# A hybrid decoder layer: the output projection split after six recurrent pairs, and the decode state update moved into the second feed-forward

## The chip, the cores and the metric

The kernel runs on one core of a Trainium2 chip. Its engines work side by side, each with its own in-order queue: TensorE (matmuls; PE in the profile, PEld its weight loads), the vector engine (DVE), the scalar engine (ACT), GpSimd (POOL) and SyncE (SP), which here issues nearly all transfers from HBM. The metric is the device time of one execution in microseconds; lower is better.

## What is computed

One layer is applied to 256 prompt tokens and to 8 decode tokens, 264 columns in all, with a model width of 2048:

```
x = x + 0.5 * swiglu(rmsnorm(x), first feed-forward)      # width 5504
proj = rmsnorm(x) @ w_in
o_att  = sliding-window attention, 16 heads, 4 key/value heads
o_rwkv = RWKV-7 time mixing, 16 heads of 64
x = x + concat(o_att, o_rwkv) @ w_out                     # 2048 x 2048
x = x + 0.5 * swiglu(rmsnorm(x), second feed-forward)
y = rmsnorm(x)
```

For the 8 decode tokens each RWKV head holds a 64 x 64 state that is read, updated once and returned:

```
sa = S @ (-kk)
S  = S * exp(logw) + outer(sa, kk * a) + outer(v, k)
```

The read `sa` and the head's output are needed for `o_rwkv`; the new S is only an output of the layer (`new_wkv_sample`).

## The kernel before

Everything is float32. A matmul is made exact enough by splitting each operand into a rounded part `hi` and a rest `lo`: three matmuls of 128x128 weights against 128x264 activations per tile (hi*hi, hi*lo, lo*hi). Weights come as chunks of up to four k-tiles, 128x512 (`chunk`, called by `gemm`): SP loads `raw` (L122, ring of 6), ACT rounds it to `hi` (L123), the vector engine subtracts to `lo` (through the helper at L58; rings of 4 for `hi` and `lo`). A chunk of four k-tiles feeds 12 matmuls. The helpers `tt` (L58), `stt` (L61), `ts` (L65), `act` (L68) and `mm` (L74) issue most instructions, so their lines stand for many places in the code.

Each feed-forward goes through its 43 blocks of 128 hidden columns in six parts of 8, 7, 7, 7, 7 and 7 (`PARTS`). A part first computes gate and up for its blocks (96 matmuls a block), then adds its share of the down projection for all 16 output tiles. After each block the vector engine evacuates two accumulators, ACT takes SiLU, and POOL does a product and a subtraction of 128x264 (the vector engine does them for the last block of a part).

The mixing stage (`mixing_body`) streams `w_in` and drives many generators, the tasks, between its chunks: `gemm` calls `tick` after each chunk, and every task then issues its next step. There are tasks for the preparation of each of eight recurrent head pairs (`prep`), for the chain of each batch of two pairs (`chain`), for each pair of attention heads (`attend`), for the decode attention (`dec_attend`), and for the decode state update (`dec_state`). The results of the eight pairs and of the eight attention tiles are 16 k-tiles of the output projection, in `mixed`.

The output projection runs in two passes over its 16 output tiles. `PASS` names the k-tiles of each pass: pairs 0 to 7, then attention tiles 8 to 15. Before a pass `drain` advances the tasks until those that it needs are done; in the first pass the attention tasks go on between its chunks. Each pass adds its result to the residual `xr`, and each k-tile is split into `hi` and `lo` by `split` (even tiles subtract on POOL, odd ones on the vector engine). Before the last `drain` the eight decode columns of the attention tiles are copied in by POOL (L824).

`dec_state` is spawned before the first pass. It transposes the decode vectors out of `XD` (matmuls `m<-C,XD`) into `XR`, and then goes through the 64 x 64 states of all heads in 16 blocks of 128x256: load a block of S on SP, five operations of 128x256 (two on POOL, three on the vector engine), store it on SP (L684). `drain([dst])` waits for it at the end of mixing.

The order in each engine's queue isn't the program's order. The tile layer takes all operations with their dependencies and builds each queue with a planner that plays the work through on its own clock: an operation that is ready there, on an engine that is free there, goes in, with earlier program order and `high_priority` first. Weight chunks and splits have high priority.

Of the kernel before, what the change touches and what calls it, by code (L numbers as in the profile page):

```python
# [7 lines left out]
F32 = mybir.dt.float32  # L8
# [5 lines left out]
P = 128  # L14
# [22 lines left out]
LKV = 26  # L37
SEQ = [('b', 0), ('b', 1), ('b', 2), ('b', 3), ('kv', 0), ('kv', 1), ('kv', 2), ('kv', 3), ('q', 0), ('q', 1), ('q', 2), ('q', 3), ('q', 4), ('q', 5), ('q', 6), ('q', 7)]
NSO = (12, 13)
PASS = [[0, 1, 2, 3, 4, 5, 6, 7], [8, 9, 10, 11, 12, 13, 14, 15]]  # L40

VG1, VGM, VG2, VGF = 0, 16, 32, 48
VMU, VKK, VKA, VA0, VRK, VLW, VLB, VSK, VSD = 64, 90, 98, 106, 114, 122, 130, 138, 154
# [4 lines left out]
def body(tc, I, O):  # L48
# [8 lines left out]
    def tt(e, out, a, b, op):  # L57
        return e.tensor_tensor(out=out, in0=a, in1=b, op=op)  # L58
# [11 lines left out]
    def bc(ap, shape):  # L70
        return ap.broadcast_to(list(shape))

    def mm(out, lhsT, rhs, start=True, stop=True, **k):
        TE.matmul(out, lhsT, rhs, start=start, stop=stop, **k)  # L74
# [8 lines left out]
    def drain(only, hold=()):  # L83
        while any(g in only for g in tasks):
            tick(hold)

    def spawn(g):
        tasks.append(g)
        return g
# [5 lines left out]
    with ExitStack() as ctx:  # L95
# [10 lines left out]
        def tmp(shape=(P, T), dt=F32):  # L106
            pool, n = cur[0]
            return pool.tile(list(shape), dt, tag="t", bufs=n, name=uid("t"))
# [4 lines left out]
        def mp():  # L113
            return pp.tile([P, 512], F32, tag="m", bufs=NM, name=uid("m"))
# [87 lines left out]
        def copy_one():  # L202
            n, c, b = copies.pop()
            tc.keep_in_program_order(A.dma_start(O[n][b, 0:127, :], I[c][b, 1:128, :]))

        def ffn(nrm, xr, gu, dn, nxt, load, begin=False):
            rstd = None
            f0 = 0
            for pi, nf in enumerate(PARTS):
                hs = [None] * nf  # L210
                late = []
                if begin:
                    early(pi)
                first = pi == 0
                if first:
                    banks = [acc() for _ in range(NACC)] + [mp() for _ in range(NM)]
                    n0 = len(banks) // 2
                    for k in range(CH):
                        load(k)
                    for k0 in range(0, KD, CH):  # L220
                        xs = nrm.xs + [None] * (KD - len(nrm.xs))
                        for i, ps in enumerate(banks):
                            gemm(ps, gu[i // 2, i % 2], xs, rng=(k0,), ahead=False)
                            if i >= len(banks) - CH and k0 + CH < KD:
                                load(k0 + CH + i - len(banks) + CH)
                    for f in range(n0):
                        raw = [tmp(), tmp()]
                        V.tensor_copy(raw[0], banks[2 * f][:, :T])
                        A.copy(raw[1], banks[2 * f + 1][:, :T])
                        late.append((f, *raw))  # L230
                for f in range(f0 + n0 if first else f0, f0 + nf):
                    pgu = [acc(), acc()]
                    if first and f == n0:
                        sq = iter(range(KD))

                        def step():
                            for k in [x for _, x in zip(range(2), sq)]:
                                nrm.square(xr[k], k % 2, True)
                    else:
                        step = None  # L240
                    if begin and pi and copies:
                        copy_one()
                    for ps, w in zip(pgu, (gu[f, 0], gu[f, 1])):
                        gemm(ps, w, nrm.xs, step)
                    last = f == f0 + nf - 1
                    if rstd is None:
                        rstd = nrm.rstd(tmp())
                    late.append((f, *(x[:, :T] for x in pgu)))
                    now = [late.pop()]
                    for _ in range(len(late) if last else min(len(late), 2 if first and f == n0 + 1 else 1)):  # L250
                        now.append(late.pop(0))
                    for j, pg, pu in now:
                        E = V if last else G
                        g = tmp()
                        tt(V, g, pg, rstd, ALU.mult)
                        s = tmp()
                        act(s, g, AF.Silu)
                        u = tmp()
                        tt(V, u, pu, rstd, ALU.mult)
                        tt(E, u, u, s, ALU.mult)  # L260
                        hi, lo = tmp(dt=F32R), tmp(dt=F32R)
                        A.copy(hi, u)
                        tt(E, lo, u, hi.bitcast(F32), ALU.subtract)
                        hs[j - f0] = (hi, lo)
                if pi == len(PARTS) - 1:
                    nrm.xs = None
                for o in range(KD):
                    ps = acc()
                    gemm(ps, dn[o, :, f0 * P:(f0 + nf) * P], hs)
                    stt(xr[o], ps[:, :T], 0.5, xr[o], ALU.mult, ALU.add)  # L270
                    if pi == len(PARTS) - 1:
                        nxt(o)
                f0 += nf
# [19 lines left out]
                    xr += [xg[:, j] for j in range(4)]  # L293
                ffn(n1, xr, I["gu1"], I["dn1"], nxt, load, True)

        def mixing(n2, n3):
            with tc.tile_pool(name="mx", bufs=1) as mx:
                cur[0] = (mx, NT)
                return mixing_body(mx, n2, n3)

        def mixing_body(mx, n2, n3):
            def fix(shape, name):
                return mx.tile(list(shape), F32, name=name)

# [3 lines left out]
            def load(src, shape):  # L308
                t = ring(shape, "ld", NLD)
                SP.dma_start(t, src)  # L310
                return t
# [1 line left out]
            ident, bo, cm = C[:, CID:CID + P], C[:, CBO:CBO + P], C[:, CCM:CCM + P]  # L313
            tri, msk = C[:, CTR:CTR + P], C[:, CMK:CMK + P]
            shc = fix((P, NSH, NB + 1), "shc")
            XD = fix((P, 8, NPAIR, NB), "XD")
            wc = fix((P, NPAIR, 4), "wc")
            tw = fix((65, T), "tw")
            G.memset(tw[64:65, :], 1.0)
# [6 lines left out]
            ts(V, nmu, mu, -1.0, ALU.mult, 1.0, ALU.add)  # L326
            tt(V, ss, ss, bc(mu.unsqueeze(2), (P, NSH, NB)), ALU.mult)
            qd = fix((P, 2, NB, 4), "qd")
            XR = fix((P, 5, 64), "XR")
            nbat = len(BATCH)  # L330
            scr = [dp.tile([BATCH[b] * 16, 1024], F32, tag=f"sa{b}", name=f"sa{b}") for b in range(nbat)]
            scr2 = [dp.tile([BATCH[b] * 16, 1024], F32, tag=f"sb{b}", name=f"sb{b}") for b in range(nbat)]
# [323 lines left out]
                tt(V, y, yp[:, :T], r, ALU.mult)  # L656
                yield

            def dec_state():
                while any(g.left for g in bts):  # L660
                    yield
                ps = mp()
                for i in range(5):
                    for h in range(2):
                        r = HALF[h]
                        mm(ps[r, i * 64:i * 64 + 64], XD[r, i, :, :], ident[r, r])
                A.copy(XR, ps[:, :320].rearrange("p (c t) -> p c t", c=5))
                yield
                n = 4
                shp = (P, n, 64)  # L670

                def bj(i):
                    return bc(XR[:, i:i + 1, :], shp)

                for k in range(64 // n):
                    r = slice(k * n, k * n + n)
                    S = load(I["st"][:, r, :], shp)
                    t1, t2 = tmp(shp), tmp(shp)
                    tt(G, t1, bc(XR[:, 3, r].unsqueeze(2), shp), bj(4), ALU.mult)
                    tt(V, S, S, bj(1), ALU.mult)  # L680
                    tt(V, t2, bc(XR[:, 0, r].unsqueeze(2), shp), bj(2), ALU.mult)
                    tt(V, S, S, t2, ALU.subtract)
                    tt(G, S, S, t1, ALU.add)
                    SP.dma_start(O["wkvs"][:, r, :], S)  # L684
                    yield

            kT, vT, Vt = [None] * 2, [None] * 2, [None] * 2
            kvn = [None] * 2

# [182 lines left out]
            k0 = 0  # L872
            for pi, ks in enumerate(PASS):
                drain(need(ks), att if max(ks) < 8 else ())
                if pi == 0:
                    dst = spawn(dec_state())
                with tc.high_priority():
                    for k in ks:
                        split(k)
                for o in range(KD):  # L880
                    ps = acc()
                    gemm(ps, I["wout"][o, :, k0 * P:(k0 + len(ks)) * P], [mixed[k] for k in ks], tick)
                    with tc.high_priority():
                        tt(V, xr[o], ps[:, :T], xr[o], ALU.add)
                    if pi == len(PASS) - 1 and o < CH:
                        n3.split(xr[o])
                for k in ks:
                    mixed[k] = None
                k0 += len(ks)
            drain([dst])  # L890
            return xr

        def second_ffn(n3, xr):
            fin = Norm(VGF, 3)

            def load(k):
# [3 lines left out]
            with tc.tile_pool(name="f2", bufs=1) as fp:  # L900
# [7 lines left out]
                        act(rt[:, 7:8], fin.sums[0][0][0:88, 0:1], AF.Sqrt)  # L908
                    act(ys[o // 4][:, o % 4], xr[o], AF.Copy, scale=vc(VGF + o))

                ffn(n3, xr, I["gu2"], I["dn2"], nxt, load)
                p = fin.sums[0]
                sm, rp = mp(), mp()
                for i, q in enumerate(p):
# [13 lines left out]
        xsp = [dp.tile([P, T], F32, tag=f"xsp{o}", name=f"xsp{o}") for o in range(KD)]  # L928
        n2, n3 = Norm(VGM), Norm(VG2)
        first_ffn(n2)  # L930
        second_ffn(n3, mixing(n2, n3))


OUTS = dict(yT=(P, KD, T), kp=(2, P, P), vp=(2, P, P), ks=(NB, P, 256), vs=(NB, P, 256),
# [97 lines left out]
```

## Time and profile before

| | us |
|---|---|
| median of 3 runs | 2045.23 (2044.63 to 2045.34) |
| the profiled execution | 2046.14 |
| its span, first to last instruction | 2042.8 |
| TensorE busy in it | 2008.5 |
| vector engine busy | 1309.7 |
| ACT busy | 1051.8 |
| POOL busy | 284.8 |

In the span the first feed-forward comes first, then the mixing stage, whose last part from about 1149 to 1275 us is the output projection, and then the second feed-forward up to the end. The mean granted TensorE clock is 0.993 of full speed. In the profile's rows `acc` and `m` are PSUM banks, `raw`, `hi` and `lo` the weight chunks, `s`, `o` and `t` activations and temporaries, `ld` a ring for small loads, in which the state blocks S stand too. A busy TensorE is counted from modelled ends of pipelined matmuls, so its gaps tell more than its busy share.

### The profile page before, as it was taken

Reading aid. Unit: us, or ns where it says so; the run is one execution under the profiler, and the core shown is the slowest. Engines: PE = TensorE matmul, PEld = TensorE weight load, DVE = VectorE, ACT = ScalarE, POOL = GpSimd, SP = SyncE. Lnnn points to the kernel's source line nnn. Section 1 sums busy time; section 2 is a strip of 40 time slices with the busy share of each in tenths; the row PEclk is TensorE's granted clock in tenths of the full one; section 3 lists DMA queues with packets and bytes.
Section 4 is the critical chain, followed back from the end, with each engine's and each line's share of the span. In section 5 each row is a group of like instructions: output and inputs, shape, how many; then the busy total and the mean of one; then the engine's idle time right before and its main releaser. Section 6 shows DMA issues by size and latency. Waiting matters only on the chain.

```text
span 2042.8 us, 45689 instructions
## 1 busy us (share of the span) xinstructions
PE 2008.5 (98%) x17198; PEld 1969.8 (96%) x17198; DVE 1309.7 (64%) x2597; ACT 1051.8 (51%) x2061; POOL 284.8 (14%) x369
## 2 busy tenths in 40 slices
PE   9999999999999999999999899999999999999997
PEld 9999999999999999999898789999999999999997
DVE  5865555655555586678768797675555555655555
ACT  5644444444444466765554644564444444444445
POOL 0401001020110222211110051030101102010012
PEclk9999999999999999999999999999999999999998
DMA  6566565655556576454454366565555555655554
GB/s 227 178 186 198 181 194 187 187 184 175 187 171 191 182 214 196 139 142 119 124 145 124 118 186 218 175 183 181 181 176 186 175 186 181 181 181 176 187 175 142
DMA packets 226989, 358.39 MB, mean 175 GB/s; under 512 B 42304, under 2 KB 80208, under 8 KB 226768
## 3 DMA queue, kind: packets, MB, share of 16 engines
q1 hardware_dynamic: 220464, 346.81, 54.6%
q10 hardware_dynamic: 6304, 8.67, 1.3%
q8 instruction: 134, 2.20, 0.4%
q14 instruction: 87, 0.71, 0.1%
HBM read 347.25 MB, written 10.21 MB: 175 GB/s over the span
## 4 chain that ended last, share of the span: by engine, by line
PE 91%; DVE 3%; DMA 2%; issue 1%; ACT 1%; SPq 1%; POOL 0%; DVEq 0%; ACTq 0%; POOLq 0%
PE acc L74 83%; PE m L74 8%; DVE lo L58 1%; DMA out_wkvs<-ld 0%; DMA raw<-in_gu 0%; DMA Xt<-sa 0%; DMA sb<-Xt 0%; DVE ld L58 0%; DVE TT L58 0%; ACT L68 0%; DMA raw<-in_win 0%; DVE st L58 0%; DMA sa<-gm 0%; ACT t L68 0%; DVE Xt L58 0%
## 5 line engine op out<-in xcount | busy, mean ns | idle before, releaser
L58 DVE TENSOR_TENSOR lo<-raw,hi 128x512 fp32r<-128x512 f32 (+1 forms) x1288 | 875.1, 683 | 578.6 <-ACT hi L123 555.9
L74 PE MATMUL acc<-s,hi 128*128 128x264 f32 x6588 | 1224.6, 286 | 4.6 <-DVE sta L65 2.8
L123 ACT CAST hi<-raw 128x512 fp32r<-128x512 f32 (+1 forms) x1288 | 776.0, 607 | 849.4 <-PE acc L74 763.7
L74 PEld LDWEIGHTS acc<-s,hi 128*128 128x128 f32 x6588 | 1025.8, 189 | 12.4 <-issue 7.1
L74 PE MATMUL acc<-s,lo 128*128 128x264 f32 x3294 | 940.6, 286 | 6.5 <-DVE lo L58 6.4
L74 PEld LDWEIGHTS acc<-s,lo 128*128 128x128 f32 x3294 | 620.4, 189 | 10.7 <-DVE lo L58 8.8
L74 PE MATMUL acc<-t,hi 128*128 128x264 f32 x2752 | 502.9, 284 | 0.0
L74 PEld LDWEIGHTS acc<-t,hi 128*128 128x128 f32 x2752 | 426.3, 188 | 0.0
L74 PE MATMUL acc<-t,lo 128*128 128x264 f32 x1376 | 388.8, 284 | 0.0
L58 POOL TENSOR_TENSOR t<-t,t 128x264 f32<-128x264 f32 (+1 forms) x148 | 157.4, 1063 | 1141.2 <-ACT hi L123 789.9
L74 PEld LDWEIGHTS acc<-t,lo 128*128 128x128 f32 x1376 | 258.4, 188 | 0.0
L58 DVE TENSOR_TENSOR t<-acc,t 128x264 f32<-128x264 f32 x156 | 67.4, 432 | 35.5 <-PE acc L74 35.1
L58 POOL TENSOR_TENSOR o<-o,o 128x264 f32<-128x264 f32 x43 | 36.3, 845 | 223.3 <-ACT o L68 216.6
L74 PE MATMUL acc<-o,hi 128*128 128x264 f32 x324 | 62.5, 284 | 0.0
L74 PE MATMUL m<-s,hi 128*128 128x264 f32 x300 | 55.9, 285 | 0.8 <-ACT hi L123 0.8
L68 ACT ACT_TABLE_LOAD x40 | 51.3, 1283 | 2.3 <-PEq L1024 1.2
L61 DVE SCALAR_TENSOR_TENSOR s<-acc,s 128x264 f32<-128x264 f32 x96 | 40.6, 427 | 15.5 <-PE acc L74 15.1
L74 PEld LDWEIGHTS acc<-o,hi 128*128 128x128 f32 x324 | 50.5, 188 | 0.0
L74 PEld LDWEIGHTS m<-s,hi 128*128 128x128 f32 x300 | 46.5, 188 | 1.0 <-ACT hi L123 1.0
L61 DVE SCALAR_TENSOR_TENSOR x<-acc,x 128x264 f32<-128x264 f32 x96 | 40.5, 426 | 10.0 <-PE acc L74 9.6
L74 PE MATMUL acc<-o,lo 128*128 128x264 f32 x162 | 46.2, 285 | 0.0
L74 PE MATMUL m<-s,lo 128*128 128x264 f32 x150 | 42.6, 284 | 0.2 <-DVE lo L58 0.2
(233 smaller groups left out, 1149.5 us busy)
## 6 DMA issues: line engine op xcount, KB each, us to landing
raw<-in_gu SPq DMA_DIRECT2D x688, 256.0 KB, 3.2
raw<-in_dn SPq DMA_DIRECT2D x224, 256.0 KB, 2.8
raw<-in_win SPq DMA_DIRECT2D x152, 256.0 KB, 3.4
raw<-in_dn SPq DMA_DIRECT2D x160, 192.0 KB, 2.7
raw<-in_wout SPq DMA_DIRECT2D x64, 256.0 KB, 3.7
xsp<-x ACTq DMA_DIRECT2D x16, 132.0 KB, 3.4
s<-xsp SPq DMA_DIRECT2D x16, 132.0 KB, 2.7
ld<-in_sT SPq DMA_DIRECT2D x16, 128.0 KB, 3.6
```

The lines of the kernel that those rows point to most:

```text
L58: return e.tensor_tensor(out=out, in0=a, in1=b, op=op)
L61: return V.scalar_tensor_tensor(out=out, in0=a, scalar=s, in1=b, op0=op0, op1=op1)
L68: return A.activation(out=out, in_=in_, func=f, **k)
L74: TE.matmul(out, lhsT, rhs, start=start, stop=stop, **k)
L123: A.copy(hi[:, :w], raw[:, :w])
```

## The change

Three things are changed. The first pass of the output projection takes pairs 0 to 5 and the second takes pairs 6 and 7 with all eight attention tiles. `dec_state` is no task of mixing any more: it is a generator that the second feed-forward advances by one step before each gate/up block of its parts 2 to 6 (`side`), with all five operations of a state block on the vector engine, the loads and stores on SP, and a ring of nine buffers of its own (`sd`), three per state block. `XD` moves to a pool that lives through both stages.

```
-PASS = [[0, 1, 2, 3, 4, 5, 6, 7], [8, 9, 10, 11, 12, 13, 14, 15]]
+PASS = [[0, 1, 2, 3, 4, 5], [6, 7, 8, 9, 10, 11, 12, 13, 14, 15]]
...
-        def ffn(nrm, xr, gu, dn, nxt, load, begin=False):
+        def ffn(nrm, xr, gu, dn, nxt, load, begin=False, side=None):
...
                     if begin and pi and copies:
                         copy_one()
+                    if side and pi:
+                        next(side, None)
                     for ps, w in zip(pgu, (gu[f, 0], gu[f, 1])):
                         gemm(ps, w, nrm.xs, step)
...
+        def dec_state(fp, XD):
+            XR = fp.tile([P, 5, 64], F32, name="XR")
+            ps = mp()
+            for i in range(5):
+                for h in range(2):
+                    r = HALF[h]
+                    mm(ps[r, i * 64:i * 64 + 64], XD[r, i, :, :], C[r, CID:CID + P][:, r])
+            A.copy(XR, ps[:, :320].rearrange("p (c t) -> p c t", c=5))
+            yield
...
+            for k in range(64 // n):
+                r = slice(k * n, k * n + n)
+                S, t1, t2 = (fp.tile(list(shp), F32, tag="sd", bufs=9, name=uid("sd")) for _ in range(3))
+                SP.dma_start(S, I["st"][:, r, :])
+                yield
+                tt(V, t1, bc(XR[:, 3, r].unsqueeze(2), shp), bj(4), ALU.mult)
+                tt(V, S, S, bj(1), ALU.mult)
+                tt(V, t2, bc(XR[:, 0, r].unsqueeze(2), shp), bj(2), ALU.mult)
+                tt(V, S, S, t2, ALU.subtract)
+                tt(V, S, S, t1, ALU.add)
+                yield
+                SP.dma_start(O["wkvs"][:, r, :], S)
...
-            def dec_state():
-                while any(g.left for g in bts):
-                    yield
...
-                    S = load(I["st"][:, r, :], shp)
-                    t1, t2 = tmp(shp), tmp(shp)
-                    tt(G, t1, bc(XR[:, 3, r].unsqueeze(2), shp), bj(4), ALU.mult)
-                    tt(V, S, S, bj(1), ALU.mult)
-                    tt(V, t2, bc(XR[:, 0, r].unsqueeze(2), shp), bj(2), ALU.mult)
-                    tt(V, S, S, t2, ALU.subtract)
-                    tt(G, S, S, t1, ALU.add)
-                    SP.dma_start(O["wkvs"][:, r, :], S)
-                    yield
...
-                if pi == 0:
-                    dst = spawn(dec_state())
...
-            drain([dst])
             return xr
...
-                ffn(n3, xr, I["gu2"], I["dn2"], nxt, load)
+                side = dec_state(fp, XD)
+                ffn(n3, xr, I["gu2"], I["dn2"], nxt, load, False, side)
```

More of the change, by code (lines that the diff above doesn't have):

```diff
@@ L294, in first_ffn, with bj, mixing, mixing_body @@
                 ffn(n1, xr, I["gu1"], I["dn1"], nxt, load, True)
-        def mixing(n2, n3):
+        def dec_state(fp, XD):
[7 more added lines that the diff above has]
+            yield
+            n = 4
+            shp = (P, n, 64)
+            def bj(i):
+                return bc(XR[:, i:i + 1, :], shp)
+            for k in range(64 // n):
[10 more added lines that the diff above has]
+                SP.dma_start(O["wkvs"][:, r, :], S)
+        def mixing(n2, n3, XD):
             with tc.tile_pool(name="mx", bufs=1) as mx:
                 cur[0] = (mx, NT)
-                return mixing_body(mx, n2, n3)
-        def mixing_body(mx, n2, n3):
+                return mixing_body(mx, n2, n3, XD)
+        def mixing_body(mx, n2, n3, XD):
             def fix(shape, name):
@@ L315, in mixing_body @@
             shc = fix((P, NSH, NB + 1), "shc")
-            XD = fix((P, 8, NPAIR, NB), "XD")
             wc = fix((P, NPAIR, 4), "wc")
@@ L328, in mixing_body @@
             qd = fix((P, 2, NB, 4), "qd")
-            XR = fix((P, 5, 64), "XR")
             nbat = len(BATCH)
@@ L657, in gnorm @@
                 yield
-            def dec_state():
-                while any(g.left for g in bts):
-                    yield
[L662 to L667, printed above, removed]
-                yield
[L669 to L676, printed above, removed]
-                    S = load(I["st"][:, r, :], shp)
-                    t1, t2 = tmp(shp), tmp(shp)
-                    tt(G, t1, bc(XR[:, 3, r].unsqueeze(2), shp), bj(4), ALU.mult)
-                    tt(V, S, S, bj(1), ALU.mult)
-                    tt(V, t2, bc(XR[:, 0, r].unsqueeze(2), shp), bj(2), ALU.mult)
-                    tt(V, S, S, t2, ALU.subtract)
-                    tt(G, S, S, t1, ALU.add)
-                    SP.dma_start(O["wkvs"][:, r, :], S)
-                    yield
             kT, vT, Vt = [None] * 2, [None] * 2, [None] * 2
@@ L889, in mixing_body, with second_ffn @@
                 k0 += len(ks)
-            drain([dst])
             return xr
-        def second_ffn(n3, xr):
+        def second_ffn(n3, xr, XD):
             fin = Norm(VGF, 3)
@@ L909, in nxt @@
                     act(ys[o // 4][:, o % 4], xr[o], AF.Copy, scale=vc(VGF + o))
-                ffn(n3, xr, I["gu2"], I["dn2"], nxt, load)
+                side = dec_state(fp, XD)
+                ffn(n3, xr, I["gu2"], I["dn2"], nxt, load, False, side)
+                assert next(side, side) is side
                 p = fin.sums[0]
@@ L930, in body @@
         first_ffn(n2)
-        second_ffn(n3, mixing(n2, n3))
+        with tc.tile_pool(name="dx", bufs=1) as dx:
+            XD = dx.tile([P, 8, NPAIR, NB], F32, name="XD")
+            second_ffn(n3, mixing(n2, n3, XD), XD)
 OUTS = dict(yT=(P, KD, T), kp=(2, P, P), vp=(2, P, P), ks=(NB, P, 256), vs=(NB, P, 256),
```

## The prediction

> **What bounds the kernel now.** I read the page's parts 1 and 4 first, then TensorE's waits between 1149 and 1275 us (the output projection), then the same stretch in windows, then the vector engine's own order of time.
>
> ```profile
> PE 2008.5 (98%) x17198; PEld 1969.8 (96%) x17198; DVE 1309.7 (64%) x2597; ACT 1051.8 (51%) x2061; POOL 284.8 (14%) x369
> ...
> PE 91%; DVE 3%; DMA 2%; issue 1%; ACT 1%; SPq 1%; POOL 0%; DVEq 0%; ACTq 0%; POOLq 0%
> ```
> ```profile
> PE acc L74 <- DVE lo L58: 3.8, 4, 1.4
> PE m L74 <- DMA ld<-in_cv: 0.2, 1, 0.2
> ```
> ```profile
> 1148.93:1166.90 17.97, 17.97 (x118) 15.18 (x116) 13.91 (x48) 10.37 (x32) 1.79 (x3) 0.94 0.36 109
> 1166.90:1186.00 19.10, 19.10 (x162) 17.18 (x162) 12.67 (x46) 9.13 (x28) 3.12 (x7) 1.00 0.53 157
> 1186.00:1204.28 18.28, 18.04 (x141) 15.94 (x139) 18.14 (x38) 6.56 (x15) 12.73 (x16) 1.00 0.68 211
> 1204.28:1212.00 7.72, 6.83 (x56) 6.62 (x56) 7.66 (x19) 3.80 (x9) 4.12 (x11) 1.00 0.38 114
> 1212.00:1222.50 10.50, 7.57 (x55) 6.71 (x55) 10.49 (x15) 3.28 (x7) 8.60 (x10) 1.00 0.61 177
> 1222.50:1232.00 9.50, 9.41 (x77) 9.20 (x76) 9.50 (x19) 3.42 (x6) 3.94 (x5) 1.00 0.88 256
> ...
> 1250.00:1274.00 24.00, 24.00 (x200) 24.00 (x200) 15.04 (x25) 10.09 (x17) 0.00 (x0) 1.00 0.57 193
> ```
>
> TensorE is the bound: its matmuls are the same before and after, so only its gaps can change. The columns of the windows are length, then busy us of PE, PEld, DVE, ACT and POOL, clock, DMA share and GB/s. In the output projection TensorE stands still for 0.24 + 0.89 + 2.93 + 0.09 = 4.15 us, all between 1186 and 1232 us, where the vector engine is busy 45.8 of 46.0 us. The four long gaps wait for a `lo` subtraction, 3.8 us. What fills the vector engine there is the decode state update:
>
> ```profile
> 1198.24 6.65 DVE L58 TENSOR_TENSOR t<-XR 128x256 f32<-128x256 f32 x9
> 1204.82 1.10 DVE L58 TENSOR_TENSOR lo<-raw,hi 128x512 fp32r<-128x512 f32 x1
> 1205.84 0.41 DVE L58 TENSOR_TENSOR ld<-ld,XR 128x256 f32<-128x256 f32 x1
> 1206.17 0.41 DVE L58 TENSOR_TENSOR t<-XR 128x256 f32<-128x256 f32 x1
> 1206.51 0.41 DVE L58 TENSOR_TENSOR ld<-ld,XR 128x256 f32<-128x256 f32 x1
> 1206.85 0.42 DVE L58 TENSOR_TENSOR s<-acc,s 128x264 f32<-128x264 f32 x1
> 1207.19 0.74 DVE L58 TENSOR_TENSOR ld<-ld,XR 128x256 f32<-128x256 f32 x2
> 1207.86 0.67 DVE L58 TENSOR_TENSOR lo<-raw,hi 128x512 fp32r<-128x512 f32 x1
> 1208.46 0.45 DVE L58 TENSOR_TENSOR t<-m,t 64x64 f32<-64x64 f32 x2
> ...
> 1213.20 0.97 DVE L58 TENSOR_TENSOR s<-o,s 128x264 fp32r<-128x264 f32 x1
> ```
> ```profile
> 1196.78 8.59 POOL L58 TENSOR_TENSOR t<-XR 128x256 f32<-128x256 f32 x11
> ```
>
> From start to start a state operation takes 0.335 us, an add of a result 0.34, a `lo` 0.60 us. While POOL runs the same kind of work, nine state operations take 6.65 us (0.74 each) and a `lo` 1.10: each POOL operation costs the vector engine about 0.40 us.
>
> **Six pairs first.** The built order of all five engines is unchanged up to the first output-projection work: the last batch's recurrent chain still stands in TensorE's queue ahead of the first pass. So the wait that a shorter first pass might have skipped stays:
>
> ```profile
> 1144.29 1.16 PE L74 MATMUL m<-sgl,ld 128*128 128x264 f32 x2 [3.73 <-ACT t L68]
> ```
>
> Gain there: nothing. The chunking changes from 64 chunks of four k-tiles to 48 of four and 32 of two. The vector engine pays 48 x 0.60 + 32 x 0.335 = 39.5 us instead of 38.4, and SP issues 16 more loads; neither is the bound. But the four `hi`/`lo` buffers now hold 36 matmuls of the first pass instead of 48: 4.3 us of cover instead of 5.8, at 0.120 us each (20.00 us for 167 below). If the softmaxes on ACT and DVE outlast it, TensorE waits for `lo`. Bounds: 0 (no wait before 1204 us now, except 0.2 for `cv`) and 5 us (as above, 3.8 us, plus one more wait of 1.4). I take 0.3, near the first, because this part of the vector queue now has no state work.
>
> **Then two pairs and all attention.** The last attention matmul was followed by 144 matmuls of the first pass (17 us); now by 39 (4.7 us). After it come:
>
> ```profile
> 1208.97 3.06 POOL L824 COPY o<-t 128x8 f32<-128x8 f32 x8 [3.60 <-DVE t L58]
> ...
> L58 POOL TENSOR_TENSOR s<-o,s 128x264 fp32r<-128x264 f32 x4 | 4.3, 1081 | 2.7 <-ACT hi L123 2.7
> ```
>
> Vector add 0.45, eight copies 3.06, four POOL splits of 1.08: the first split is ready 0.2 + 0.45 + 3.06 + 1.08 = 4.8 us after the last attention matmul, the fourth 8.0. TensorE wants them after 4.7 us, 0.4 us of attention matmuls, and 7 or 25 matmuls of the new pass: 5.9 and 8.1 us. Cost 0 to 3 us (four splits one after the other without cover); I take 0.3.
>
> **State update out of the projection.** Its 48 vector and 32 POOL operations leave the stretch where TensorE lost 4.15 us; every one of those gaps has state work just ahead of it or, for `cv`, its loads in the same ring. SP loses 16 loads, 16 stores and their waits there. Gain 4.1 us; bounds 0 and 4.4 (a little slack between matmuls beside the gaps). The transposes move with it, at the same price:
>
> ```profile
> 1166.92 0.80 PE L74 MATMUL m<-C,XD 64*64 64x64 f32 x20
> ```
>
> **State update into the second feed-forward.** In the source one step is taken per gate/up block of parts 2 to 6, 35 blocks. The built order doesn't keep that: the scheduler fills the vector engine's idle slots, and all 80 operations (the 32 of POOL are now vector work too) stand between two `lo` of the second part, with only 36 `lo` and 9 evacuations among them:
>
> ```
> L58 TensorTensor lo_20189 ... 8 state operations ... lo_20207, 2 state, lo_20225, 2 state, lo_20243, ...
> ```
>
> Now this place looks like this:
>
> ```profile
> 1400.00:1420.00 20.00, 20.00 (x167) 20.00 (x166) 12.28 (x20) 8.21 (x15) 0.00 (x0) 1.00 0.57 178
> 1420.00:1440.00 20.00, 20.00 (x167) 20.00 (x166) 11.18 (x18) 9.80 (x17) 2.46 (x3) 1.00 0.51 180
> ```
>
> TensorE needs a `lo` every 12 x 0.120 = 1.444 us, so 36 take 52.0 us. The vector engine's work is 80 x 0.335 + 36 x 0.60 + 9 x 0.345 = 51.5 us: just enough, with nothing over. The head start is four buffers. Counted from the stretch's beginning, the 24th chunk's `lo` starts at 0.7 + 52 x 0.335 + 19 x 0.60 + 5 x 0.345 = 31.2 us and must start by 32.7; the 29th at 38.0, by 40.0. Headroom 1.5 to 2.0 us. Two things eat it:
>
> ```profile
> L58 DVE TENSOR_TENSOR lo<-raw,hi 128x512 fp32r<-128x512 f32 x295 | 204.1, 692 | 185.0 <-ACT hi L123 180.5
> ...
> L58 POOL TENSOR_TENSOR t<-t,t 128x264 f32<-128x264 f32 x24 | 29.5, 1229 | 429.3 <-ACT hi L123 301.7 <-DVE t L58 127.6
> L58 POOL TENSOR_TENSOR t<-t,t 128x264 fp32r<-128x264 f32 x24 | 22.3, 931 | 12.6 <-ACT t L262 12.6
> ...
> DMA to landing us min/median/max: 1.7/2.8/5.1
> ...
> DMA to landing us min/median/max: 2.1/3.1/4.1
> ```
>
> First, POOL's two operations per block: now the vector engine has gaps for them (`lo` stays at 0.69); with none left each costs it 0.40, so 6 cost 2.4 us by the 29th chunk. Second, the ring of nine state buffers: five of the 16 loads wait on SP until an earlier store has landed (the last two rows: stores, then state loads). Store and load take 2.8 + 3.1 = 5.9 us, and the vector engine comes round in about 6.4, less what SP is held up. A late load stops the vector engine and every `lo` behind it, and SP's wait holds the weight loads queued behind it, which have six buffers (8.7 us). I count 0.4 us for each of the early four, about 1.5. So 2.4 + 1.5 against 1.5 to 2.0: TensorE loses some 2 to 2.5 us. Bounds: 0, if headroom holds; and the worst rate shown, 3.82 us of 18.22 between 1204.28 and 1222.50, over 52 us: 10.9. I take 2.5, near the first, because only POOL's splits and chunks of state work together made the worst rate; the whole saturated stretch, 4.15 of 46.0 us, would give 4.7.
>
> [...]
>
> **Sum.** -4.1 + 0.3 + 0.3 + 2.5 = -1.0 us. The profiled execution took 2046.14 us (span 2042.8), so 2045.1 by its own measure; against the median 2045.23 that is 2044.2. A measurement tells about 0.2%, 4.1 us.
>
> **Rivals.** (a) The update hides wholly and the passes cost nothing: -4.1, 2041.1. For it: TensorE at 20.00 of 20.00 and a vector engine at 11 to 12 of 20. Against it: 99% load in one stretch. (b) Slower: the packed stretch runs as badly as 1204 to 1222 us did, 10.9 us, from state loads that come late and POOL's turns; 2045.2 - 4.1 + 0.6 + 10.9 = 2052.6. It decides once the stretch costs over 7.6 us. For it: saturation and a store-to-load round of 5.9 us; against it: 28 us of the old saturated stretch cost only 0.3. (c) The first pass, with less cover, waits for `lo` through the softmaxes: 5 us instead of 0.3, and 2048.9. (d) The moved work doesn't change the total: gaps only change place, 2045.2; this lies inside my own range. (e) A POOL operation holds the vector engine for its whole 0.93 us, not 0.40: six cost 5.6 us instead of 2.4, and the time is 2047.4. For it: some operations beside POOL's splits stretched from 0.43 to 0.97 us; against it: the 0.74 us pairs.
>
> **Numbers.** Forecast with (d), 2042 to 2046.5: 0.48; (e) 0.10, within 0.2% still. (a): 0.15, half of it beyond 0.2%. (b): 0.17, (c): 0.10, half of it beyond. Faster 0.08, within 0.2% 0.70, slower 0.22. The range 2041.0 to 2050.5 leaves out the worst of (b) and little below (a).
>
> **What would show it.** No TensorE wait for `lo` between 1186 and 1235 us, and a first pass without new gaps; the matmuls up to 1148 us unchanged; a stretch of some 52 us from about 1410 us with the vector engine at 19 to 20 of 20 and TensorE gaps there for `lo`, 2 to 3 us in all; state loads named as what the vector engine waits for. Wrong would be a vector engine at 13 to 14 of 20 spread over all of the second feed-forward, gaps of over 7 us there, or waits for `lo` before 1200 us.

## The result and the profile after

The changed kernel takes 2050.81 us in the median (8 runs, 2048.99 to 2053.82) against 2044.95 us of the kernel before beside it: ratio 1.0027, 95% interval 1.0019 to 1.0036. It is slower by 5.9 us, 0.3 us above the top of the predicted range; rival (b), 2052.6 us, is the case that came. Its profiled execution took 2051.9 us, with a span of 2050.1.

The page's parts 1 and 4 of the changed kernel look almost like those of before, which is why they can't tell the story:

```profile
PE 2014.3 (98%) x17198; PEld 1974.0 (96%) x17198; DVE 1312.7 (64%) x2645; ACT 1054.3 (51%) x2077; POOL 254.1 (12%) x337
...
PE 91%; DVE 3%; DMA 3%; SPq 1%; ACT 1%; issue 1%; DVEq 0%; ACTq 0%
```

Three kinds of TensorE rows occur at the same places in both programs and cut the span into stages: the last `m<-sgl,ld` of the recurrent chain (the output projection begins), the first row of the second feed-forward's norm (`m<-o,ones`), and the last norm (`m<-ones,o`). First the kernel before, then the changed one, in order of time (start, length, both in us):

```profile
1146.27 1.25 PE L74 MATMUL m<-sgl,ld 128*128 128x264 f32 x2 [0.82 <-DVE t L749]
...
1332.67 1.05 PE L74 MATMUL m<-o,ones 128*128 128x264 f32 x4
...
2029.07 0.56 PE L74 MATMUL m<-ones,o 128*88 128x1 f32 x6
```
```profile
1147.24 1.25 PE L74 MATMUL m<-sgl,ld 128*128 128x264 f32 x2 [3.73 <-ACT t L68]
1149.22 1.25 PE L74 MATMUL m<-sgl,ld 128*128 128x264 f32 x2 [0.73 <-DVE t L749]
...
1329.23 1.05 PE L74 MATMUL m<-o,ones 128*128 128x264 f32 x4
...
2037.42 0.56 PE L74 MATMUL m<-ones,o 128*88 128x1 f32 x6
```

From start to start the projection falls from 186.4 to 180.0 us and the second feed-forward grows from 696.4 to 708.2 us: -6.4 and +11.8. The rest of the difference between the two spans is 2.9 us more ahead of the projection (1146.27 to 1149.22) and about 1 us less after the last norm. The 2.9 us can't be put down to the change: that row begins at 1149.22 and at 1147.15 us in two executions of the changed kernel, and at 1148.46 and 1152.06 in two of the spread kernel below.

In the projection the waits for `lo` are gone. TensorE's waits from 1149 to 1290 us in the changed kernel:

```profile
PE m L74 <- DVE t L749: 0.7, 1, 0.7
```

The loss stands where the state update went. The windows of the changed kernel (the columns are those of the prediction):

```profile
1420.00:1430.00 10.00, 10.00 (x85) 10.00 (x84) 9.36 (x22) 4.82 (x9) 0.81 (x1) 1.00 0.74 229
1430.00:1440.00 10.00, 9.33 (x75) 8.91 (x74) 9.14 (x21) 4.22 (x9) 0.97 (x1) 1.00 0.56 175
1440.00:1450.00 10.00, 8.78 (x69) 8.41 (x69) 9.62 (x22) 4.33 (x8) 2.10 (x2) 1.00 0.70 218
1450.00:1460.00 10.00, 8.65 (x68) 8.01 (x66) 7.66 (x18) 2.91 (x6) 0.80 (x2) 1.00 0.66 201
1460.00:1470.00 10.00, 8.46 (x63) 7.93 (x64) 6.76 (x16) 3.49 (x7) 1.44 (x1) 1.00 0.58 160
1470.00:1480.00 10.00, 8.85 (x66) 8.00 (x65) 8.95 (x18) 4.80 (x9) 2.11 (x2) 1.00 0.77 249
1480.00:1490.00 10.00, 10.00 (x84) 10.00 (x83) 5.50 (x10) 5.16 (x9) 2.02 (x2) 1.00 0.76 244
```

Read the counts of matmuls before the busy times. An undisturbed window has 84; the five from 1430 to 1480 us have 75 + 69 + 68 + 63 + 66 = 341 instead of 420, so some 79 are missing, 9.5 us at 0.120 us each. And the vector engine is not full there: 6.76 to 9.62 of 10 us. The waits of TensorE, the vector engine and SP's queue from 1400 to 1480 us say why:

```profile
PE acc L74 <- DVE lo L58: 5.7, 9, 1.5
PE acc L74 <- ACT hi L123: 0.2, 1, 0.2
```
```profile
DVE sd L58 <- DMA sd<-in_st: 6.7, 6, 2.7
DVE lo L58 <- ACT hi L123: 3.8, 5, 0.8
DVE sd L58 <- DMA out_wkvs<-sd: 2.2, 3, 1.6
```
```profile
SPq L316 <- DMA out_wkvs<-sd: 16.8, 6, 4.0
SPq L122 <- DVE sd L58: 13.9, 19, 2.4
```

The vector engine stands still for 6.7 + 2.2 = 8.9 us for state loads and for stores that have not landed, with the `lo` subtractions queued behind. SP stands for 16.8 us in front of state loads whose buffer is still being stored, with weight loads queued behind. Stores take longer here than the 2.8 us of the prediction; of the tile `out_wkvs`:

```profile
DMA to landing us min/median/max: 2.0/4.0/4.8
```

Two measures of one loss differ: TensorE's shown waits add to 5.9 us, the missing matmuls to 9.5. A row shows the reason:

```profile
1457.29 0.41 PE L74 MATMUL acc<-o,hi 128*128 128x264 f32 x2
1457.99 0.39 PE L74 MATMUL acc<-o,lo 128*128 128x264 f32 x1 [0.29 <-DVE lo L58]
1458.22 0.40 PE L74 MATMUL acc<-o,hi 128*128 128x264 f32 x2
```

The second matmul of the first row begins at about 1457.41. Two starts later, at 0.120 us each, it should be 1457.65; it is 1458.22. A shown wait of 0.29 us has cost 0.57: the profile counts a matmul as busy to its modelled end, and from the matmul after the wait to the next start it is 0.23 us here instead of 0.120.

### The profile page after: what moved, and what is told of

Read it like the earlier page. It is cut to its first block, busy times and chain, and to the rows that moved or that the text cites. A ratio compares the mean times of both kernels' runs of the same rounds, so it can differ in the third digit from the quotient of the medians.

```text
span 2050.1 us, 45723 instructions
## 1 busy us (share of the span) xinstructions
PE 2014.3 (98%) x17198; PEld 1974.0 (96%) x17198; DVE 1312.7 (64%) x2645; ACT 1054.3 (51%) x2077; POOL 254.1 (12%) x337
## 4 chain that ended last, share of the span: by engine, by line
PE 91%; DVE 3%; DMA 3%; SPq 1%; ACT 1%; issue 1%; DVEq 0%; ACTq 0%
PE acc L74 83%; PE m L74 8%; DVE lo L58 1%; DMA out_wkvs<-sd 1%; DMA raw<-in_gu 1%; DMA Xt<-sa 0%; DMA sd<-in_st 0%; SPq L532 0%; ACT t L68 0%; DMA sa<-gm 0%; DVE sd L58 0%; SPq L533 0%; DVE uv L600 0%; DMA sb<-Xt 0%; DVE st L58 0%
## 5 line engine op out<-in xcount | busy, mean ns | idle before, releaser
L58 DVE TENSOR_TENSOR lo<-raw,hi 128x512 fp32r<-128x512 f32 (+2 forms) x1304 | 875.0, 674 | 575.9 <-ACT hi L123 549.4
L123 ACT CAST hi<-raw 128x512 fp32r<-128x512 f32 (+2 forms) x1304 | 779.0, 602 | 860.9 <-PE acc L74 769.3
```

Of the source, the lines that this page charges most:

```text
L123: A.copy(hi[:, :w], raw[:, :w])
```

## The experiments

The stages are measured between the three rows above, each in one profiled execution; the times are medians beside the kernel before on the same chip. The kernel before took 2044.95 us beside the changed kernel and between 2046.88 and 2047.69 beside the others, so rows are better compared by their ratios.

| kernel | us | ratio, 95% interval | projection | second feed-forward |
|---|---|---|---|---|
| before | | | 186.4 | 696.4 |
| changed | 2050.81 | 1.0027 (1.0019 to 1.0036) | 180.0 | 708.2 |
| changed, again | 2050.75 | 1.0024 (1.0014 to 1.0034) | 179.8 | 706.6 |
| passes alone | 2052.12 | 1.0020 (1.0010 to 1.0030) | 191.8 | 696.8 |
| move alone | 2053.29 | 1.0024 (1.0011 to 1.0036) | 178.3 | 706.6 |
| 48 state buffers | 2054.21 | 1.0032 (1.0023 to 1.0042) | 180.3 | 710.3 |
| the same, POOL's work on the vector engine | 2049.84 | 1.0009 (0.9999 to 1.0018) | 179.8 | 705.2 |
| packed, S ring of 3 | 2049.12 | 1.0014 (1.0004 to 1.0023) | 179.8 | 706.4 |
| packed, S ring of 16 | 2046.24 | 0.9996 (0.9987 to 1.0005) | 180.0 | 702.3 |
| spread, six pairs first | 2043.83 | 0.9980 (0.9970 to 0.9989) | 179.8 | 698.7 |
| spread, again | 2043.60 | 0.9981 (0.9972 to 0.9990) | 180.3 | 698.7 |
| spread, old passes | 2041.45 | 0.9974 (0.9963 to 0.9984) | 182.5 | 698.7 |
| spread, old passes, again | 2041.08 | 0.9970 (0.9958 to 0.9982) | 182.6 | 698.7 |
| no state update | 2040.27 | 0.9964 (0.9951 to 0.9977) | 179.8 | 696.8 |

The first two runs take the change apart. **The passes alone**, in the kernel before:

```
-PASS = [[0, 1, 2, 3, 4, 5, 6, 7], [8, 9, 10, 11, 12, 13, 14, 15]]
+PASS = [[0, 1, 2, 3, 4, 5], [6, 7, 8, 9, 10, 11, 12, 13, 14, 15]]
```

> The kernel before with nothing changed but the passes of the output projection: pairs 0 to 5 first, then pairs 6 and 7 with all attention; the state update stays in mixing. Prediction's theory: the order of the passes is worth +0.3 and +0.3 us, so 2045.0 + 0.6 = 2045.6 us, with the same waits for lo of about 4 us in the projection, only elsewhere. Rival 1 (the six-pair pass itself gives the gain of the projection, 6.4 us between the anchors of the two traces): 2038.6. Rival 2 (four buffers cover 4.3 us instead of 5.8 and the state work still stands there): 2049 or more.

It is 4.4 us above the kernel before beside it (2047.69), as much as the second rival says and not the 0.6 us of the prediction; the first rival, that the passes make the projection faster, is out. TensorE's waits from 1149 to 1290 us, then two windows of the projection:

```profile
PE acc L74 <- DVE lo L58: 4.3, 2, 2.2
PE acc L74 <- POOL s L58: 1.8, 1, 1.8
```
```profile
1210.00:1220.00 10.00, 5.17 (x33) 4.25 (x32) 9.92 (x22) 4.33 (x12) 7.62 (x15) 0.81 0.54 160
1220.00:1230.00 10.00, 8.72 (x53) 8.72 (x54) 10.00 (x19) 3.10 (x6) 6.61 (x7) 0.68 0.53 161
```

and the same windows of the kernel before:

```profile
1210.00:1220.00 10.00, 6.72 (x48) 5.87 (x48) 9.97 (x17) 4.66 (x11) 10.00 (x15) 1.00 0.55 161
1220.00:1230.00 10.00, 9.46 (x78) 9.24 (x76) 10.00 (x18) 4.04 (x7) 4.29 (x5) 1.00 0.80 237
```

The second pass does wait for POOL's first split here (1.8 us). Three waits of about 2 us stand in these 20 us, and the granted clock is 0.81 and 0.68 instead of 1.00: 86 matmuls in 20 us instead of 126. This is one profile; the close waits and the lower clock stand side by side in it, and that the one brings the other was not tested.

**The move alone**, in the changed kernel:

```
-PASS = [[0, 1, 2, 3, 4, 5], [6, 7, 8, 9, 10, 11, 12, 13, 14, 15]]
+PASS = [[0, 1, 2, 3, 4, 5, 6, 7], [8, 9, 10, 11, 12, 13, 14, 15]]
```

> The changed kernel with the old passes (pairs 0 to 7, then attention): only the state update is moved. If the move carries both the gain in the projection and the loss in the second feed-forward, and the passes are worth under 1 us: 2050.8 plus or minus 1, with the second feed-forward 11.8 us longer than before and the projection 5 to 6.4 us shorter. If the passes give the projection's gain: the projection keeps its old length and the time is 2055 to 2057.

The ratio, 1.0024, is that of the changed kernel, and the stages are of the kind that the first case expected: the projection falls by 8.1 us, a little more than the 5 to 6.4, and the second feed-forward grows by 10.2. The move carries both the gain and the loss. But the profiled execution was the fastest of its ten, 2046.76 us against a median of 2053.29, so these stage lengths, the 8.1 us above all, belong to a lucky execution.

**The state update spread out.** Here the steps are held to the program's order, so that one state block falls on two gate/up blocks (`keep` on the two transfers likewise):

```
+            keep = tc.keep_in_program_order
...
-                tt(V, t1, bc(XR[:, 3, r].unsqueeze(2), shp), bj(4), ALU.mult)
-                tt(V, S, S, bj(1), ALU.mult)
+                keep(tt(V, t1, bc(XR[:, 3, r].unsqueeze(2), shp), bj(4), ALU.mult))
+                keep(tt(V, S, S, bj(1), ALU.mult))
...
```

> The changed kernel, but each state operation, load and store is pinned behind what the program issues before it on its engine, so that one state block is taken per two gate/up blocks over all of parts 2 to 6 instead of all in one stretch of 36 lo. Theory (the packing is what costs): the 11.8 us of the second feed-forward go but for about 1 us, the projection keeps its gain: 2050.8 - 11 = 2039.8, range 2038.5 to 2042. Rival (the moved work costs wherever it stands: 16 loads and 16 stores on the queue of the weight loads, 80 vector operations): waits spread over the stage, 2047 to 2051.

The same 80 operations, 16 loads and 16 stores, on the same engines and with the same nine buffers, now cost the second feed-forward 2.3 us over before instead of 11.8. TensorE has no row with a wait from 1400 to 2020 us, and the stretch that was packed looks like this:

```profile
1420.00:1440.00 20.00, 20.00 (x166) 20.00 (x165) 12.12 (x21) 9.73 (x17) 3.86 (x4) 1.00 0.53 170
1440.00:1460.00 20.00, 20.00 (x166) 20.00 (x165) 11.88 (x20) 9.51 (x17) 2.19 (x2) 1.00 0.67 204
```

So the packing is the cost, not the work. The kernel is faster than before, by 3.9 us. What in the packing costs, the next four runs ask.

**Many buffers.** The changed kernel with `tag="sd", bufs=48` instead of `bufs=9`:

> The changed kernel with 48 state buffers instead of nine: no state load waits for a store any more, and the planner packs the same 80 operations among 22 lo instead of 36. Theory A (the round from store to load, with SP standing still in it, made the loss): the vector engine's waits for sd go, and what is left is throughput: 80 x 0.335 + 22 x 0.60 + 5 x 0.345 = 41.7 us of vector work where TensorE wants 22 lo in 31.8 us, with 5.8 us of buffers, so 4 us lost instead of 11.8, up to 6 with POOL's turns: 2043 to 2045. Theory B (the vector engine is saturated and its operations are stretched beside POOL and the transfers): a denser packing loses more than 11.8 us, 2051 to 2055.

Theory A fell in this form: no state operation waits any more, and the stage is longer still, 710.3 us. Theory B has the time right but not the reason: the vector operations keep their lengths (0.42 us for a state operation, 0.68 for a `lo`). TensorE now waits for ACT, ACT for POOL (each from 1400 to 1480 us), and two POOL operations, of a kind that took 1.23 us in the kernel before, look like this:

```profile
PE acc L74 <- ACT hi L123: 7.4, 4, 5.2
```
```profile
ACT t L264 <- POOL t L58: 8.7, 2, 6.3
```
```profile
1433.97 7.56 POOL L58 TENSOR_TENSOR t<-t,t 128x264 f32<-128x264 f32 x1 [71.17 <-DVE t L58]
...
1450.34 6.57 POOL L58 TENSOR_TENSOR t<-t,t 128x264 f32<-128x264 f32 x1 [7.54 <-DVE t L58]
```

In these 7.56 us the vector engine ran without a break, all of it state operations and `lo` subtractions but for one evacuation at 1440.85 us; a window out of their middle:

```profile
1435.00:1440.00 5.00, 2.83 (x22) 2.60 (x21) 5.00 (x15) 0.22 (x1) 5.00 (x1) 1.00 0.88 292
```

POOL's product was done only at the end, ACT stood in front of the product for 6.3 us with the `hi` casts of the weights queued behind, and TensorE ran dry, for up to 5.2 us at a time.

**The same with POOL's two operations per block on the vector engine**, in the second part:

```
-                        E = V if last else G
+                        E = V if last or (side and pi == 1) else G
```

> The run with 48 state buffers, but the product and the subtraction of each gate/up block of the second part stand on the vector engine instead of POOL. If POOL's operations of 7.56 and 6.57 us beside the packed vector work were what TensorE waited for (5.2 us, through ACT's hi): those waits go though the vector engine now has some 6 more operations in the stretch, and the second feed-forward falls from 710.3 to 701 to 704 us; the time by 6 to 9 us. If throughput of the vector engine is the cause: 6 x 0.34 = 2 us longer, 712 or more.

TensorE's waits from 1400 to 1480 us and one window:

```profile
PE acc L74 <- DVE lo L58: 2.3, 5, 0.5
PE acc L74 <- ACT hi L123: 1.0, 3, 0.3
```
```profile
1430.00:1440.00 10.00, 8.65 (x65) 7.92 (x64) 10.00 (x27) 3.51 (x6) 0.00 (x0) 1.00 0.77 237
```

The wait for ACT falls from 7.4 to 1.0 us and the stage from 710.3 to 705.2 us, although the vector engine has more to do. That shows the path through POOL. The stage ends 1 us above the forecast, and the time falls by 0.0023 of the kernel before, 4.7 us, instead of 6 to 9. What remains goes with a vector engine that has too much work in one place: it is busy without a gap in all four windows from 1420 to 1460 us, and TensorE waits for `lo`.

**The ring at a fixed density.** The state update is written anew: S has a ring of its own of 3 (below) or 16 buffers, loads are asked for two blocks ahead, and the vector operations are pinned to one state block per two weight chunks.

```
+            def fetch(k):
+                S = fp.tile(list(shp), F32, tag="sS", bufs=3, name=uid("sS"))
+                SP.dma_start(S, I["st"][:, k * n:k * n + n, :])
+                Ss.append(S)
...
-                    if side and pi:
-                        next(side, None)
+                    if side and pi:
+                        step = lambda: next(side, None)
```

> The changed kernel with its packed state update written anew so that its density is fixed: one state block per two weight chunks of the second part (pinned on the vector engine), S in a ring of three blocks of its own, loads asked for two blocks ahead, as many waits of a load for a store as in the changed kernel. 80 state operations stand among 37 lo. Theory A (the store-to-load round holds the vector engine and SP): it loses about what the changed kernel loses in the second feed-forward, 8 to 12 us over the 696.4 of before, and the vector engine waits some 6 to 9 us for state loads and stores there. Theory B (density alone): 51.5 us of vector work for 37 x 1.444 = 53.4 us, so it should lose no more than 2 us.

> The same with 16 buffers for S, so that no load waits for a store; 80 state operations among 34 lo, so slightly denser than with three. Theory A: the waits for state loads go and the second feed-forward is within 3 us of before plus 0.9 for the moved transposes, so 5 to 8 us less than with the ring of three. Theory B: as long as with three or longer. Theory C (what held TensorE in the run with 48 buffers: POOL's product does not get through beside an unbroken train of vector operations, ACT waits for it ahead of its hi casts): single POOL operations of several us, and TensorE waits for hi, 3 us or more each time the train has no gap.

With three buffers the vector engine waits, from 1400 to 1480 us, as in the changed kernel; with 16 it no longer waits for a state load:

```profile
DVE sS L58 <- DMA sS<-in_st: 7.7, 8, 1.9
DVE lo L58 <- ACT hi L123: 4.6, 6, 0.8
```
```profile
DVE lo L58 <- ACT hi L123: 12.0, 13, 1.6
```

The second feed-forward falls from 706.4 to 702.3 us though the packing is a little denser, and the median time by 2.9 us. So the round from store to load is worth about 4 us of it net, a little under the 5 to 8 us of theory A, and with 16 buffers the stage doesn't come within the 3 us that theory A left. (With three buffers 13 state loads stand on SP for a store, 24.2 us in all; in the changed kernel it was 6 and 16.8 us, so the two are not alike in this.) The rest follows theory C in a milder form: POOL's products last up to 4.96 us, ACT waits 13.7 us for them, TensorE only 1.7 us for ACT.

```profile
1438.61 4.96 POOL L58 TENSOR_TENSOR t<-t,t 128x264 f32<-128x264 f32 x1 [7.81 <-DVE t L58]
```

The 702.3 us are still 5.5 above a kernel without the update, so a dense packing costs more than theory B's arithmetic allowed, even where no load is late.

**A second look** on one chip, with the changed kernel, both spread versions and the floor. The spread version with the old passes differs from the first only in `PASS`; the floor leaves out the two lines that advance `side`, so the new decode state is not written.

> The spread state update with the old passes of the output projection. If the passes of six and ten cost 1.7 us in the projection and about 1 us in the last batch's chain, as the run of the move alone beside the changed kernel says: 2 to 3 us below the spread run with six pairs, some 6 us below before (ratio 0.997). If the passes are worth nothing: the same as the spread run, ratio 0.998.

> The changed kernel itself, on the same chip as the next three, so that the spread versions can be set beside it: ratio to before 1.0027 again (1.0019 to 1.0036), and the loss of 11 to 12 us in the second feed-forward beside a gain of about 6 us in the projection.

> Spread state update, old passes. Theory (the passes of six and ten are worth nothing or cost a little): ratio 0.997, 0.0005 or more below the version with six pairs. Rival (the difference of the first two runs was chance): both 0.9975 to 0.998.

> Spread state update, passes of six and ten. The same as the run before within 0.0005 if the passes are worth nothing; 0.001 above it (2 us) if the shorter first pass costs what the single profiles show in the projection and in the last batch's chain.

> The changed kernel with the state update left out altogether (no transposes, state loads, operations or stores; the new decode state is not written). It is the floor for any placing of that work. If the spread update hides wholly but for its ten transposes, this is 1 us or less below the spread version with six pairs (ratio 0.9975 to 0.998), and its second feed-forward is 696.4 us as before; if the 2.3 us that the spread version shows over before in that stage are a cost of the spread work, it is 2 us or more below.

The spread update with the old passes beats both kernels, twice: 2041.45 and 2041.08 us. It lies below the version with six pairs by 0.0006 of the kernel before (two chips, 1.2 us) and by 2.5 us (on one chip), but the intervals overlap, and in the profiles its projection is longer (182.5 against 179.8 us; from 1200 to 1210 us its granted clock is 0.50 against 0.83, with 45 matmuls against 62): whether the passes of six and ten cost anything once the state update is gone stays open. The changed kernel repeats its ratio, 1.0024. Without any state update the time is 2040.27 us, 3.3 us below the spread version with six pairs, again with intervals that overlap. The second feed-forward takes 696.8 us there and 698.7 in all four spread profiles, so even spread the update costs 1.9 us of that stage: the second case of the last expectation. No row names a wait for it; the ten transposes, 20 rows of matmuls that took 0.80 us in the kernel before, are part of it, the rest can't be placed.

## Why the prediction was wrong

**Six pairs first.** Right that the 3.73 us wait stays; the row is there unchanged. The cover of four buffers was enough in the changed kernel, and the attention splits came in time: no wait, where the prediction had put 0.3 and 0.3. Both terms hold only because the state update was gone. With it in place the same passes cost 4.4 us, among them the 1.8 us wait for POOL's split, inside the bound of 0 to 3 that was given.

**State update out of the projection.** The mechanism was right and its size too small. The prediction took 4.1 us, with 4.4 as the most; measured are 6.4 us in the changed kernel, 0.8 us of it the transposes. With the old passes it is 8.1 us in the profile of the move alone and 3.9 and 3.8 in the two spread profiles, where the granted clock from 1200 to 1210 us is 0.50 and 0.59 (last section). The term was read from shown waits. Read from counts, the same stretch gives more. From 1186 to 1232 us, first the kernel before, then the move alone:

```profile
1186.00:1232.00 46.00, 41.84 (x322) 38.48 (x321) 45.79 (x89) 17.06 (x36) 29.38 (x39) 1.00 0.65 196
```
```profile
1186.00:1232.00 46.00, 46.00 (x379) 44.76 (x378) 30.82 (x60) 22.16 (x45) 4.58 (x12) 1.00 0.55 166
```

57 matmuls more, and 57 x 0.120 is 6.8 us: that is what the state work cost there. The changed kernel has 363 in the same 46 us, at a clock of 0.96, and the spread kernel with the old passes has 45 from 1200 to 1210 us at 0.50, where the move alone has 81 at 1.00: part of the gain is lost again to the clock.

**State update into the second feed-forward.** This step failed: 2.5 us predicted, 10.2 to 11.8 measured in the stage, some 0.8 us of it the transposes. The prediction had the place, the packing, the saturation and both culprits; the term that it had far too small is that of the late state loads. Its three pieces:

- The state loads: "0.4 us for each of the early four, about 1.5". Measured 8.9 us of waits of the vector engine. The store lands after 4.0 us, not 2.8, so store and load take 7.0 us and a round of about 6.4 is too short; and while SP waits for the store, the loads behind it start late too, so the delays don't stay with one block. The pair of rings prices this at about 4 us of TensorE's time, net of what POOL then loses.
- POOL's turns: "six cost 2.4" of the vector engine, 0.40 each. This was nearly right. Of the eight POOL operations from 1428 to 1476 us of the changed kernel six lengthen one vector operation by 0.54 to 0.57 us and one by 0.10, 3.4 us in all. The first two, POOL and then the vector engine, where a `lo` alone takes 0.68 and two state operations 0.75:

```profile
1428.83 0.81 POOL L58 TENSOR_TENSOR t<-t,t 128x264 f32<-128x264 f32 x1 [68.16 <-DVE t L58]
1430.16 0.97 POOL L58 TENSOR_TENSOR t<-t,t 128x264 fp32r<-128x264 f32 x1 [0.52 <-ACT t L264]
```
```profile
1428.93 1.25 DVE L58 TENSOR_TENSOR lo<-raw,hi 128x512 fp32r<-128x512 f32 x1
1430.11 1.31 DVE L58 TENSOR_TENSOR sd<-sd,sd 128x256 f32<-128x256 f32 x2
```

- The headroom of 1.5 to 2.0 us: the late state loads alone exceed it.

With the measured terms the prediction's own sum gives 8.9 + 3.4 less 1.5 to 2.0, so 10.3 to 10.8 us. This is an estimate, since waits may overlap, but it has the size of the measured loss. It is not a price list: where the late loads were taken away (48 and 16 buffers), POOL's products lasted up to 7.56 and 4.96 us instead, with ACT and then TensorE behind them, and 5.5 us or more stayed.

The worst rate of the kernel before was in the quoted lines, 10.9 us by shown waits. By counts it was (56 + 55) matmuls in 18.22 us where 152 fit, so 4.9 us lost there and 14 over 52 us; the measured 9.5 us in the windows from 1430 to 1480 lie between that and the 2.5 chosen. The reason given for choosing low, that "only POOL's splits and chunks of state work together made the worst rate", was not one that a row had shown.

**The rivals.** Rival (b) came: 2052.6 against 2050.8, with late state loads and POOL's turns as named; its 10.9 us meets the 10.2 to 11.8 of the stage in part by luck, since it is the rate of another place, 1204 to 1222 us of the kernel before, where the vector engine has no row with a wait. Rivals (a) and (d) are excluded by the time and the stages, (c) by the missing waits in the projection. Rival (e) is not what happened: in the changed kernel a POOL operation (0.75 to 1.48 us there) costs the vector engine 0.57 us at most, not its whole length, and in the kernels with 48 and 16 buffers it is POOL's operation that grows beside the vector engine's: not by one vector instruction but by a train of them, up to 7.56 and 4.96 us in all, where it took 1.23 us in the kernel before. What makes the two engines lengthen each other's operations was not shown; no run here varied the operands.

## What to carry to other kernels

Work that is free on average is not free where a scheduler puts it: 80 operations that fit into gaps over 518 us cost 10 to 12 us in one stretch of 65, and pinning them to the program's order turned a slower kernel into a faster one. Count matmuls per window against an undisturbed window instead of adding shown waits, both for what a stretch loses now and for what it would gain. A ring that is written back needs buffers for store landing plus load landing under the traffic of that stage (4.0 and 3.0 us here, against a round of about 6.4), or its loads block the queue that they share with the weights (for 16.8 us here); but more buffers alone can make things worse, as the run with 48 shows (710.3 us in the stage instead of 708.2), if they let the planner pack the work still closer.

## What had not been expected of the hardware

**A half clock without a gap.** Two kernels with the same passes in the projection, the move alone and the spread version with the old passes, in the same window, with no wait of TensorE shown in either:

```profile
1200.00:1210.00 10.00, 10.00 (x81) 9.65 (x82) 8.03 (x14) 5.94 (x14) 3.81 (x11) 1.00 0.38 107
```
```profile
1200.00:1210.00 10.00, 10.00 (x45) 9.26 (x45) 3.35 (x7) 3.08 (x8) 2.04 (x9) 0.50 0.19 47
```

Granted clock 1.00 against 0.50, 81 matmuls against 45, 4.3 us. Just ahead of it both run 24 narrow matmuls of the decode attention in 2.74 us, here in the spread version:

```profile
1195.76 2.74 PE L74 MATMUL m<-t,ld 128*128 128x8 f32 x24
```

The two profiles have these matmuls in common, but not the clock after them. What lowers it was not shown: no run varied the number of these matmuls. A lowered clock is no rare case there: of the eight profiles without the state update in the projection whose clock was read in this window, the move alone is the only one at 1.00, and the other seven lie at 0.50 to 0.90. The changed kernel is among the seven:

```profile
1200.00:1210.00 10.00, 10.00 (x64) 8.27 (x64) 2.88 (x7) 2.69 (x7) 2.04 (x9) 0.83 0.31 94
```

So the same passes with the same work took 178.3 and 182.5 us in the projection: a single profile can't price a change of 0.2% in that stage.

**POOL beside a train of vector work.** The two long POOL operations of the run with 48 buffers (7.56 and 6.57 us) ended 0.7 us after the vector engine's next evacuation of an accumulator (`t<-acc,t`) began; with 16 buffers four lasted 3.56 to 4.96 us and ended 0.6 to 0.7 us after the vector engine's first gap, or again after such an evacuation had begun. Why POOL's operations ended just then was not tested, nor why those of the changed kernel took no more than 1.48 us.
